# A conv layer's norm shift takes its matmul banks two tiles later, and VectorE's splits and gated products come ahead of its taps

## The chip, the cores and the metric

One core of a Trainium2 chip runs the whole program in one launch. The metric is the time of one execution in microseconds of the device, from a median of several; smaller is better. The engines named below are the PE (TensorE, matrix products), VectorE (DVE), ScalarE (ACT), GpSimd (POOL) and SyncE (SP, which issues the DMAs).

## What is computed

The reference is a network of a recurrent block and four mixer layers (conv, RWKV, attention, conv) on 512 tokens of 1024 channels, with a context of 256 tokens beside it in the first three. The change touches the two conv layers alone. Cut to what matters:

```python
def conv_branch(h, w_in, dw, db, ln_g, ln_b, w_out):
    a, b, gate = jnp.split(h @ w_in, 3, axis=-1)
    y = a * jax.nn.sigmoid(b)
    y = depthwise_conv(y, dw, db)            # 31 taps along the tokens, a filter for each channel
    y = jax.nn.silu(layernorm(y, ln_g, ln_b))
    return (y * jax.nn.silu(gate)) @ w_out
```

The first conv layer (layer 0) has 768 tokens, since the context goes through it too; the last one (layer 3) has 512.

## The kernel before

**Tiles.** In `conv_layer` (L693) channels lie on the 128 partitions, so 1024 channels make eight tiles `kt` = 0 to 7, and tokens run along the free dimension: W = 512 in layer 3, W = 784 in layer 0 (two spans of 256 and 512 with a gap). For each tile there are three projections (`proj`, L752): 1 for `b`, 0 for `a`, 2 for the gate. A projection loads a 1024 x 128 block of weights (`wblock`, L180), splits it into a high part on ScalarE (`whi`, L171) and a low part on VectorE (`wlo`, L174), and makes, for each of eight k, three products (L200, L201, L203) for each span. The raw weights have two buffers, `whi` and `wlo` three each.

**A tile's way.** `gated(kt)` (L762) makes the two projections, and from them y (`ypad`, with zeros at its ends, three buffers) with a tanh on ScalarE (L772) and a gated product on VectorE (L773). The 31 taps then run on VectorE (`conv_dve`, L800: L802 for the first, L805 for thirty more, each adding to the same row `cvo`), or, for the tiles in `PEK` (2, 4, 6, 7 in layer 3; 3, 6, 7 in layer 0), on the PE (`spread`, L776, which copies rows with 16 DMAs, and `conv_pe`, L788). `gate(kt)` (L757) makes the third projection and a silu.

**The shift.** The layer norm's sums are taken of values with a rough mean subtracted. This `shift` is the mean of tile 0's rows over its 128 channels, times the number of tiles over 8: one product of `cvo` with a constant (L809), after tile 0's last tap, copied by ScalarE (L811) and subtracted from each tile (L812, or within L797 for tiles on the PE). `sums_of` (L814) adds up the shifted rows and their squares on the PE, two tiles at a time.

**Order.** The order of each engine's instructions is made when the program is built: a scheduler takes the instructions as the source writes them and places each on its engine when its inputs are there. `high_priority(offset=n)` treats what is in its block as if written n instructions earlier; `wblock` uses `WPRIO` = 200. Tiles of the pool `pmm` (six banks; `self.mm()`, L129) hold all projections, the shift's product and, to the end of the loop, one bank of sums. In a projection a call takes one bank for each span.

**What fills in.** `fill` (L598), called at each `wblock`, reads and multiplies one block of the modulation weights (`mod_mul` L584, `mod_cols` L594; they use another pool of two banks). In layer 0 these belong to later layers. In layer 3 there are none left.

Of the kernel before, what the change touches and what calls it, by code (L numbers as in the profile page):

```python
# [12 lines left out]
AF = mybir.ActivationFunctionType  # L13
ALU = mybir.AluOpType
# [9 lines left out]
KT = D // P  # L24
TILES = [0, 128, 256, 384]
EPS = 1e-6
T3=0
WPRIO = 200
FB=[int(c) for c in "2221122333"]
RB=2  # L30
LB=8
# [11 lines left out]
EXP=[int(c) for c in "0001"]  # L43

NAS=[[int(c) for c in x] for x in "00001121200000 00000101000000 00000010100000".split()]
GL=2

PEK=((2,4,6,7),(3,6,7))

# [21 lines left out]
class K:  # L71
    def __init__(self, tc, ins, taps=None):
        self.tc = tc
        self.nc = tc.nc
        self.ins = ins
        self.taps = taps or {}
        self.es = ExitStack()

    def tap(self, name, ap):
        if name in self.taps:  # L80
            self.nc.sync.dma_start(self.taps[name], ap)
# [98 lines left out]
    def wblock(self, w, k0, kn, c0, nc_, eng="act"):  # L180

        n = kn * nc_
        self.fill()
        with self.tc.high_priority(offset=WPRIO):
            raw = self.raw_w()
            rv = raw[:, :n].rearrange("p (k c) -> p k c", k=kn)
            self.nc.sync.dma_start(rv, w[k0 * P:(k0 + kn) * P, c0:c0 + nc_].rearrange("(k p) c -> p k c", p=P))
            hi, lo = self.split_w(raw[:, :n], n, eng)
        return (hi[:, :n].rearrange("p (k c) -> p k c", k=kn), lo[:, :n].rearrange("p (k c) -> p k c", k=kn))
# [503 lines left out]
    def conv_layer(self, i, X, XC):  # L693
        nc, ins = self.nc, self.ins
        j = i // 3
        gs, sh, ga = self.modulation(i)
        if XC is not None:
            segs = [(XC, 2, 1), (X, 4, 0)]
            spans = [(0, 256), (256, 768)]
            offs, W = [0, 272], 784  # L700
        else:
            segs = [(X, 4, 0)]
            spans = [(0, 512)]
            offs, W = [0], 512
        lens = [b - a for a, b in spans]
        ns = len(segs)
        w_in, w_out = ins["conv_w_in_2"][j], ins["conv_w_out_2"][j]
        with ExitStack() as es:
# [5 lines left out]
            cv = yp.tile([P, KT, W], F32, name="cvo")  # L714
# [7 lines left out]
            ps = self.ptr.tile([P, 512], F32, name="tr")  # L722
# [9 lines left out]
            shift = yp.tile([P, W], F32, name="shift")  # L732
# [15 lines left out]
            with es2:  # L748
                xh, xl = (lambda k: hh[:, k, :]), (lambda k: hl[:, k, :])
                work = self.pool(es2, "cvw", bufs=2)  # L750

                def proj(sec, kt):  # L752
                    ps = [self.mm() for _ in range(ns)]
                    self.linear_fm([ps[q][:, :lens[q]] for q in range(ns)], w_in, sec * D + kt * P, xh, xl, spans)
                    return ps

                def gate(kt):  # L757
                    ps = proj(2, kt)
                    for q in range(ns):
                        nc.scalar.activation(sg[:, kt, offs[q]:offs[q] + lens[q]], ps[q][:, :lens[q]], AF.Silu)  # L760

                def gated(kt):  # L762

                    pb, pa = proj(1, kt), proj(0, kt)
                    yp_ = work.tile([P, W + 32], F32, name="ypad", bufs=3)
                    nc.gpsimd.memset(yp_[:, 0:15], 0.0)  # L766
                    if ns == 2:
                        nc.gpsimd.memset(yp_[:, 271:287], 0.0)
                    nc.gpsimd.memset(yp_[:, W + 15:W + 32], 0.0)
                    for q in range(ns):  # L770
                        y = yp_[:, 15 + offs[q]:15 + offs[q] + lens[q]]
                        nc.scalar.activation(y, pb[q][:, :lens[q]], AF.Tanh, scale=0.5)  # L772
                        nc.vector.scalar_tensor_tensor(y, y, 1.0, pa[q][:, :lens[q]], ALU.add, ALU.mult)  # L773
                    return yp_

                def spread(kt, yp_):  # L776


                    w = work.tile([P, 8, 4, 32], F32, name="wst", bufs=1)
                    nc.vector.tensor_tensor(w, dwq[:, :, :, kt].rearrange("p g m -> p m g").unsqueeze(3).to_broadcast([P, 8, 4, 32]),  # L780
                                            id32.unsqueeze(1).unsqueeze(1).to_broadcast([P, 8, 4, 32]), ALU.mult)
                    y4 = work.tile([P, 4, W + 28], F32, name="y4", bufs=1)
                    for g in range(4):
                        for q in range(4):
                            nc.sync.dma_start(y4[32 * q:32 * q + 32, g, :], yp_[32 * g:32 * g + 32, q:q + W + 28])
                    return y4, w

                def conv_pe(kt, y4, w):  # L788
                    ps = [self.mm() for _ in range(ns)]
                    for q in range(ns):  # L790
                        for m in range(8):
                            for g in range(4):
                                nc.tensor.matmul(ps[q][32 * g:32 * g + 32, :lens[q]], w[:, m, g, :],
                                                 y4[:, g, offs[q] + 4 * m:offs[q] + 4 * m + lens[q]], start=m == 0, stop=m == 7)
                    for q in range(ns):
                        sl = slice(offs[q], offs[q] + lens[q])
                        nc.vector.scalar_tensor_tensor(cv[:, kt, sl], ps[q][:, :lens[q]], self.col("conv_db_2", 8 * j + kt),  # L797
                                                       shift[:, sl], ALU.add, ALU.subtract)

                def conv_dve(kt, yp_):  # L800
                    acc = cv[:, kt, :]
                    nc.vector.tensor_scalar(acc, yp_[:, 0:W], dwh[:, 0, kt:kt + 1], self.col("conv_db_2", 8 * j + kt),  # L802
                                            ALU.mult, ALU.add)
                    for tap in range(1, 31):
                        nc.vector.scalar_tensor_tensor(acc, yp_[:, tap:tap + W], dwh[:, tap, kt:kt + 1], acc, ALU.mult, ALU.add)  # L805
                    if kt == 0:
                        ps = [self.mm() for _ in range(ns)]
                        for q in range(ns):
                            nc.tensor.matmul(ps[q][:, :lens[q]], self.inv_d, acc[:, offs[q]:offs[q] + lens[q]], start=True, stop=True)  # L809
                        for q in range(ns):  # L810
                            nc.scalar.activation(shift[:, offs[q]:offs[q] + lens[q]], ps[q][:, :lens[q]], AF.Copy, scale=float(KT))  # L811
                    nc.vector.tensor_tensor(acc, acc, shift, ALU.subtract)  # L812

                def sums_of(kt):  # L814

                    for q in range(ns):
                        rhs, sl = [], slice(offs[q], offs[q] + lens[q])
                        for k in (kt, kt + 1):
                            sq = work.tile([P, 512], F32, name="sq")
                            nc.scalar.activation(sq[:, :lens[q]], cv[:, k, sl], AF.Square)  # L820
                            rhs += [cv[:, k, sl], sq[:, :lens[q]]]
                        if kt == KT - 2 and ns == 1:

                            nc.scalar.activation(warm, sq[:, 0:1], AF.Sqrt)
                        for i, x in enumerate(rhs):
                            nc.tensor.matmul(sums[q][32 * i:32 * i + 32, :lens[q]], self.inv_d[:, 0:32], x,
                                             start=kt == 0, stop=kt == KT - 2)

                on_pe, ops = PEK[ns - 1], {}
                for kt in range(KT):  # L830
                    yp_ = gated(kt)
                    if kt in on_pe:
                        ops[kt] = spread(kt, yp_)
                    else:
                        conv_dve(kt, yp_)
                    if kt >= GL:
                        gate(kt - GL)
                    if kt - 1 in on_pe:
                        conv_pe(kt - 1, *ops[kt - 1])
                    if kt % 2 and kt > 2:  # L840
                        sums_of(kt - 3)
                gate(KT - 2)
                conv_pe(KT - 1, *ops[KT - 1])
                sums_of(KT - 2)
                gate(KT - 1)

            with ExitStack() as es2:
                op = self.pool(es2, "cvo", side="right")
# [72 lines left out]
    def rwkv_layer(self, X, XC):  # L921
# [133 lines left out]
        def feat(name, i, shape=(P, 384)):  # L1055
            return fp.tile(list(shape), F32, name=name, bufs=FB[i])

# [900 lines left out]
def build(tc, ins, out, taps=None, stages="F0123", test=None):  # L1958
    k = K(tc, ins, taps)
    nc = tc.nc  # L1960
    with k.es:
        k.setup()
        sd = dict(side="right") if stages[0] == "2" else {}
        X = k.open_stream(**sd)
        with tc.high_priority(offset=10 * WPRIO):
            for t in range(4):
# [60 lines left out]
```

## Time and profile before

| | us |
|---|---|
| median of 3 runs | 2747.01 (2746.84 to 2750.37) |
| the profiled execution | 2750.99 |
| its span, first to last instruction | 2749.3 |
| PE busy | 2401.8 (87%) |
| VectorE busy | 1696.3 (62%) |
| ScalarE busy | 1014.8 (37%) |
| GpSimd busy | 713.7 (26%) |
| mean granted PE clock | 0.919 of full speed |

The shares are means over stages with different limits; what the change is worth has to be read from the two conv layers, in time from about 400 to 860 and from about 2450 to the end. Matmuls are pipelined, so a row's duration is longer than the distance to the next row's start; the distance is what counts.

### The profile page before, as it was taken

To read this page: it belongs to the slowest core of one execution; us is meant where nothing else is said; L and a number is where in the kernel's file an instruction comes from. 1 tells how busy PE (TensorE), PEld (TensorE's weight loads), DVE (VectorE), ACT (ScalarE), POOL (GpSimd) and SP (SyncE) were. 2 spreads that over 40 slices of the span, in tenths; PEclk is the share of its full clock that TensorE was granted. 3 is DMA by queue.
4 is the path that set the end of the run, shared out by engine and by line. 5 is a ranking of instruction groups with operands and counts; after the bars stand their busy time and mean duration, and the time that the engine had idled before them with its cause. 6 is when DMAs were issued, how large, how long until landed. Compare 5 with 4: busy or idle time off the path is not lost. (4 is left out here: it accounts for less than half of the span.)

```text
span 2749.3 us, 48387 instructions
## 1 busy us (share of the span) xinstructions
PE 2401.8 (87%) x19837; PEld 1900.0 (69%) x19867; DVE 1696.3 (62%) x2577; ACT 1014.8 (37%) x1861; POOL 713.7 (26%) x700
## 2 busy tenths in 40 slices
PE   6998867999895889888699885989999899996996
PEld 4776655877574767566588774768788788874655
DVE  4434356687357588888778883545154378446836
ACT  4642342212332233233355552233333367331223
POOL 0101001000204269988222531210000287100001
PEclk9998986999997989999599997989999999997998
DMA  5523444224322327665524444432455311221331
GB/s 149 149 81 108 153 131 130 70 71 117 86 69 72 88 62 237 178 190 166 194 95 145 138 134 128 178 113 81 148 152 160 116 47 39 83 79 48 108 94 54
DMA packets 352942, 319.06 MB, mean 116 GB/s; under 512 B 19679, under 2 KB 292032, under 8 KB 352208
## 3 DMA queue, kind: packets, MB, share of 16 engines
q1 hardware_dynamic: 352720, 315.95, 38.1%
q8 instruction: 157, 2.57, 0.4%
q14 instruction: 65, 0.53, 0.1%
HBM read 241.85 MB, written 64.63 MB: 111 GB/s over the span
## 5 line engine op out<-in xcount | busy, mean ns | idle before, releaser
L174 DVE TENSOR_TENSOR wlo<-wraw,whi 128x1024 fp32r<-128x1024 f32 x212 | 267.5, 1263 | 489.6 <-ACT whi L171 478.1
L171 ACT ACTIVATE whi<-wraw 128x1024 fp32r<-128x1024 f32 x212 | 224.3, 1058 | 742.5 <-PE mm L201 404.8
L201 PE MATMUL mm<-hT_lo,whi 128*128 128x512 f32 (+1 forms) x864 | 323.2, 374 | 0.0
L200 PE MATMUL mm<-hT_hi,whi 128*128 128x512 f32 (+1 forms) x864 | 317.8, 379 | 0.8 <-ACT h L679 0.8
L203 PE MATMUL mm<-hT_hi,wlo 128*128 128x512 f32 (+1 forms) x864 | 290.4, 371 | 0.5 <-DVE wlo L174 0.5
L805 DVE SCALAR_TENSOR_TENSOR cvo<-ypad,dwh,cvo 128x784 f32<-128x784 f32 (+1 forms) x270 | 239.3, 908 | 5.6
L203 PEld LDWEIGHTS mm<-hT_hi,wlo 128*128 128x128 f32 x864 | 164.1, 190 | 40.3 <-issue 2.2
L201 PEld LDWEIGHTS mm<-hT_lo,whi 128*128 128x128 f32 x864 | 165.0, 191 | 34.9 <-issue 7.8
L200 PEld LDWEIGHTS mm<-hT_hi,whi 128*128 128x128 f32 x864 | 165.0, 191 | 34.3 <-issue 9.8
L219 PE MATMUL mm<-whi,hT_hi 128*128 128x512 f32 x384 | 152.8, 399 | 1.3 <-ACT hT_hi L264 1.3
L220 PE MATMUL mm<-wlo,hT_hi 128*128 128x512 f32 x384 | 152.4, 397 | 0.0
L221 PE MATMUL mm<-whi,hT_lo 128*128 128x512 f32 x384 | 150.2, 399 | 0.0
L766 POOL MEMSET ypad<- 128x15 f32 x16 | 1.7, 113 | 551.0 <-DVE cvo L805 215.5
L201 PE MATMUL mm<-llo,whi 128*128 128x256 f32 (+1 forms) x256 | 89.3, 370 | 10.1 <-DVE llo L274 10.0
L200 PE MATMUL mm<-lhi,whi 128*128 128x256 f32 (+1 forms) x256 | 82.7, 365 | 17.2 <-POOL lhi L273 16.0
L584 PE MATMUL tr<-mraw,sc 128*32 128x128 f32 x1536 | 72.1, 309 | 28.7 <-DMA mraw<-in_mod_w_dram 25.1
L219 PE MATMUL mm<-whi,lhi 128*128 128x512 f32 x192 | 82.5, 432 | 8.1 <-DVE so L1525 3.9
L220 PE MATMUL mm<-wlo,lhi 128*128 128x512 f32 x192 | 81.2, 423 | 5.8 <-DVE wlo L174 5.8
L219 PEld LDWEIGHTS mm<-whi,hT_hi 128*128 128x128 f32 x384 | 72.7, 189 | 18.7 <-issue 2.2
L220 PEld LDWEIGHTS mm<-wlo,hT_hi 128*128 128x128 f32 x384 | 72.6, 189 | 15.5 <-issue 1.0
L221 PEld LDWEIGHTS mm<-whi,hT_lo 128*128 128x128 f32 x384 | 71.9, 189 | 16.3 <-issue 2.2
L221 PE MATMUL mm<-whi,llo 128*128 128x512 f32 x192 | 79.8, 426 | 2.7 <-DVE llo L274 2.7
(501 smaller groups left out, 5880.4 us busy)
## 6 DMA issues: line engine op xcount, KB each, us to landing
mraw<-in_mod_w_dram SPq DMA_DIRECT2D x96, 512.0 KB
wraw<-in_conv_w_in_dram SPq DMA_DIRECT2D x48, 512.0 KB
wraw<-in_attn_w_in_dram SPq DMA_DIRECT2D x48, 512.0 KB
wraw<-in_w_in_dram SPq DMA_DIRECT2D x24, 512.0 KB
f_d<-F SPq DMA_DIRECT2D x32, 384.0 KB
ar_d<-AR SPq DMA_DIRECT2D x32, 384.0 KB
F<-f_d SPq DMA_DIRECT2D x24, 512.0 KB
AR<-ar_d SPq DMA_DIRECT2D x24, 512.0 KB
```

Of the source, the lines that this page charges most:

```text
L171: nc.scalar.activation(hi[:, :n], raw, AF.Copy)
L174: nc.vector.tensor_tensor(lo[:, :n], raw, hi[:, :n].bitcast(F32), ALU.subtract)
L200: nc.tensor.matmul(ps[s], wh[:, k, :], xh(k)[:, a:b], start=k == 0, stop=False)
L201: nc.tensor.matmul(ps[s], wh[:, k, :], xl(k)[:, a:b], start=False, stop=False)
L203: nc.tensor.matmul(ps[s], wl[:, k, :], xh(k)[:, a:b], start=False, stop=k == kts - 1)
L219: nc.tensor.matmul(ps, h, wh[:, kk, :], start=k == 0, stop=False)
L220: nc.tensor.matmul(ps, h, wl[:, kk, :], start=False, stop=False)
L221: nc.tensor.matmul(ps, l, wh[:, kk, :], start=False, stop=k == kts - 1)
L584: nc.tensor.matmul(ps[g:g + 32, 0:P], self.sc[:, k, :], raw[:, k, :], start=k < 4, stop=k >= 4)
L766: nc.gpsimd.memset(yp_[:, 0:15], 0.0)
L805: nc.vector.scalar_tensor_tensor(acc, yp_[:, tap:tap + W], dwh[:, tap, kt:kt + 1], acc, ALU.mult, ALU.add)
```

## The change

- The shift's product leaves `conv_dve(0)`. A new function `first_shift` makes it behind `gated(2)`, so behind the projections of tiles 1 and 2, one bank for each span in turn; it also subtracts the shift from tiles 0 and 1. `conv_dve` subtracts it itself only for `kt > 1`.
- `gate(0)` moves from `kt` = 2 to `kt` = 1; at `kt` = 2 there is no gate, from 3 on it is `gate(kt - 2)` as before.
- In the loop over `kt` the weight loads and splits have the priority offset 800 (`CPRIO`) in place of 200, and the tanh and the gated product (L772, L773) get it too, which had none.

```diff
+CPRIO = 800
-GL=2
-        with self.tc.high_priority(offset=WPRIO):
+        with self.tc.high_priority(offset=self.wprio):
...
-                    for q in range(ns):
-                        y = yp_[:, 15 + offs[q]:15 + offs[q] + lens[q]]
-                        nc.scalar.activation(y, pb[q][:, :lens[q]], AF.Tanh, scale=0.5)
-                        nc.vector.scalar_tensor_tensor(y, y, 1.0, pa[q][:, :lens[q]], ALU.add, ALU.mult)
+                    with self.tc.high_priority(offset=CPRIO):
+                        for q in range(ns):
+                            y = yp_[:, 15 + offs[q]:15 + offs[q] + lens[q]]
+                            nc.scalar.activation(y, pb[q][:, :lens[q]], AF.Tanh, scale=0.5)
+                            nc.vector.scalar_tensor_tensor(y, y, 1.0, pa[q][:, :lens[q]], ALU.add, ALU.mult)
...
-                    if kt == 0:
-                        ps = [self.mm() for _ in range(ns)]
-                        for q in range(ns):
-                            nc.tensor.matmul(ps[q][:, :lens[q]], self.inv_d, acc[:, offs[q]:offs[q] + lens[q]], start=True, stop=True)
-                        for q in range(ns):
-                            nc.scalar.activation(shift[:, offs[q]:offs[q] + lens[q]], ps[q][:, :lens[q]], AF.Copy, scale=float(KT))
-                    nc.vector.tensor_tensor(acc, acc, shift, ALU.subtract)
+                    if kt > 1:
+                        nc.vector.tensor_tensor(acc, acc, shift, ALU.subtract)
+
+                def first_shift():
+
+                    acc = cv[:, 0, :]
+                    for q in range(ns):
+                        ps, sl = self.mm(), slice(offs[q], offs[q] + lens[q])
+                        nc.tensor.matmul(ps[:, :lens[q]], self.inv_d, acc[:, sl], start=True, stop=True)
+                        nc.scalar.activation(shift[:, sl], ps[:, :lens[q]], AF.Copy, scale=float(KT))
+                    for kt in range(2):
+                        nc.vector.tensor_tensor(cv[:, kt, :], cv[:, kt, :], shift, ALU.subtract)
...
-                on_pe, ops = PEK[ns - 1], {}
+                on_pe, ops, self.wprio = PEK[ns - 1], {}, CPRIO
                 for kt in range(KT):
                     yp_ = gated(kt)
+                    if kt == 2:
+                        first_shift()
                     if kt in on_pe:
                         ops[kt] = spread(kt, yp_)
                     else:
                         conv_dve(kt, yp_)
-                    if kt >= GL:
-                        gate(kt - GL)
+                    if kt == 1 or kt > 2:
+                        gate(max(0, kt - 2))
```

Behind the loop `self.wprio` goes back to 200.

## Rows read from the trace of the kernel before

**Rows 1.** Windows by stage: busy us and count of each engine, clock, DMA.

```profile
core 0: us, PE busy (x) PEld busy (x) DVE busy (x) ACT busy (x) POOL busy (x), PEclk, DMA share, GB/s
443.00:487.00 44.00, 23.61 (x290) 16.46 (x290) 33.96 (x38) 5.09 (x17) 0.20 (x3) 0.53 0.69 195
487.00:735.00 248.00, 248.00 (x1628) 185.31 (x1628) 163.07 (x177) 47.37 (x82) 0.98 (x14) 0.99 0.30 80
2480.00:2510.00 30.00, 3.60 (x49) 3.02 (x38) 27.29 (x35) 3.34 (x5) 0.15 (x2) 0.56 0.13 36
2510.00:2671.00 161.00, 161.00 (x796) 108.95 (x799) 105.63 (x132) 38.22 (x48) 0.63 (x8) 0.99 0.35 98
```

**Rows 2.** Timeline, PE, layer 3: start, us, line, operands, count, [idle before, releaser].

```profile
2479.76 0.65 PE L725 MATMUL tr<-dwh,ident 128*32 128x64 f32 x32
...
2483.42 1.72 PE L639 MATMUL tr<-ident,mod 128*128 128x128 f32 x8 [1.92 <-ACT dwq L727]
2509.62 2.07 PE L809 MATMUL mm<-cvo,inv_d 128*128 128x512 f32 x2 [24.48 <-DVE cvo L805]
```

**Rows 3.** Timeline, ScalarE, layer 3: first and last of the three splits.

```profile
2457.13 1.04 ACT L171 ACTIVATE whi<-wraw 128x1024 fp32r<-128x1024 f32 x1
...
2482.04 1.05 ACT L171 ACTIVATE whi<-wraw 128x1024 fp32r<-128x1024 f32 x1
```

**Rows 4.** Timeline, PE, layer 0: the shift's product.

```profile
486.55 2.93 PE L809 MATMUL mm<-cvo,inv_d 128*128 128x256 f32 x4
```

**Rows 5.** Groups by line, PE, 443.5 to 486.5: busy, mean ns, idle before.

```profile
L584 PE MATMUL tr<-mraw,sc 128*32 128x128 f32 x244 | 16.3, 412 | 18.8 <-DMA mraw<-in_mod_w_dram 16.8 <-DVE mod L595 1.5 <-ACT mrow L585 0.5
L594 PE MATMUL tr<-msel,mrow 128*128 128x2 f32 x32 | 6.7, 330 | 1.6 <-ACT mrow L585 1.6
```

**Rows 6.** Windows of L200 alone: us, PE busy (count), clock, DMA.

```profile
2524.05:2546.36 22.31, 12.63 (x32) 1.00 0.35 92
515.09:548.80 33.71, 20.29 (x64) 1.00 0.22 63
```

**Rows 7.** Timeline, VectorE, layer 3: tile 0's taps; two tiles' taps.

```profile
2485.98 23.59 DVE L805 SCALAR_TENSOR_TENSOR cvo<-ypad,dwh,cvo 128x512 f32<-128x512 f32 x30
...
2555.62 4.07 DVE L805 SCALAR_TENSOR_TENSOR cvo<-ypad,dwh,cvo 128x512 f32<-128x512 f32 x6
```

**Rows 8.** Timeline, VectorE, layer 0: tile 0 alone; tiles 1 and 2.

```profile
444.97 0.68 DVE L802 TENSOR_SCALAR cvo<-ypad,dwh,cols 128x784 f32<-128x784 f32 x1
...
457.40 9.59 DVE L805 SCALAR_TENSOR_TENSOR cvo<-ypad,dwh,cvo 128x784 f32<-128x784 f32 x9
...
526.57 0.68 DVE L802 TENSOR_SCALAR cvo<-ypad,dwh,cols 128x784 f32<-128x784 f32 x1
...
534.03 7.65 DVE L805 SCALAR_TENSOR_TENSOR cvo<-ypad,dwh,cvo 128x784 f32<-128x784 f32 x8
...
570.24 0.97 DVE L812 TENSOR_TENSOR cvo<-cvo,shift 128x784 f32<-128x784 f32 x1
```

**Rows 9.** Windows of L805 alone, layer 0: us, VectorE busy (count).

```profile
508.00:526.50 18.50, 12.40 (x12) 1.00 0.20 58
526.50:570.30 43.80, 34.63 (x36) 1.00 0.38 99
```

**Rows 10.** Groups by line, VectorE: 498 to 676, then 2524 to 2636.

```profile
L174 DVE TENSOR_TENSOR wlo<-wraw,whi 128x1024 fp32r<-128x1024 f32 x19 | 23.2, 1223 | 16.9 <-ACT whi L171 16.7
L773 DVE SCALAR_TENSOR_TENSOR ypad<-ypad,mm 128x256 f32<-128x256 f32 (+1 forms) x14 | 7.2, 552 | 11.5 <-PE mm L203 11.5
...
L174 DVE TENSOR_TENSOR wlo<-wraw,whi 128x1024 fp32r<-128x1024 f32 x16 | 19.6, 1223 | 7.4 <-ACT whi L171 7.2
L773 DVE SCALAR_TENSOR_TENSOR ypad<-ypad,mm 128x512 f32<-128x512 f32 x6 | 4.1, 687 | 5.0 <-PE mm L203 4.6 <-DMA wraw<-in_conv_w_in_dram 0.4
```

**Rows 11.** Timeline, PE, layer 0: a modulation group at full clock.

```profile
644.62 0.64 PE L584 MATMUL tr<-mraw,sc 128*32 128x128 f32 x16
```

**Rows 12.** The page's group of all low-part splits of the kernel.

```profile
L174 DVE TENSOR_TENSOR wlo<-wraw,whi 128x1024 fp32r<-128x1024 f32 x212 | 267.5, 1263 | 489.6 <-ACT whi L171 478.1
```

More of the change, by code (lines that the diff above doesn't have):

```diff
@@ L77, in __init__ @@
         self.es = ExitStack()
+        self.wprio = WPRIO
     def tap(self, name, ap):
@@ L845, in conv_layer @@
                 gate(KT - 1)
+            self.wprio = WPRIO
             with ExitStack() as es2:
```

## The prediction

> **What bounds the kernel now.** I read the busy time by stretch first. In each of the two conv layers it shows the same picture: a stretch in which the PE is nearly idle, and behind it one in which it is never idle [rows 1]. In conv layer 0 the PE is busy 23.61 of the 44 us from 443 to 487 and then 248.00 of 248; in conv layer 3 it is busy 3.60 of 30 us from 2480 to 2510 and then 161.00 of 161. So behind the gap the PE sets the end of the layer, VectorE (163.07 of 248, 105.63 of 161) does not, and a gain can only come from the gap.
>
> Then the PE in order of time. In conv layer 3 the two projections of tile 0 end at 2479.8, some small products follow, and then the PE sits 24.48 us in front of L809, the shift's product, whose releaser is the tap line L805 [rows 2]. Tile 1's projections stand behind it, though their weights are there: three splits had been made beyond tile 0's, the last started at 2482.04 [rows 3]. Nothing else that the profile shows holds them, and at most three of the six banks are taken (one by the sums, two by tile 0). I read it so: a bank of the pool is handed out in the order of the source, so whoever asks behind the shift's product waits until that product is placed, and the PE, which takes its matmuls in order, waits with it. In conv layer 0 the same wait ends with L809 at 486.55 [rows 4]; there the modulation products (L584, L594) fill it, 15 groups of 16 matmuls in 43 us, 23.0 us busy, mostly waiting for their own DMA [rows 5].
>
> **The change, part by part.**
>
> *The product behind two tiles.* In front of it now stand pb1, pa1 (tile 1's projections), gate 0, pb2 and pa2: five projections in either layer. Their pitch is read behind the gap: a projection has eight L200 in layer 3 (one for each k) and sixteen in layer 0 (two spans), and four of them take 22.31 us with 32 L200 and 33.71 us with 64 [rows 6], so 5.58 and 8.43 us each. They are worth 27.9 us and 42.1 us of PE work that leaves the bound stretch. But the product keeps its condition, the last tap of tile 0, and the question is when that comes. Every us that it comes later than 2509.6 or 486.6 is taken off again.
>
> *Tile 0's taps now have company.* Before, VectorE ran them with no other taps around: in layer 3 30 taps from 2485.98 in 23.59 us, 0.786 us each; in layer 0 from L802 at 444.97, 1.07 us each (nine in 9.59) [rows 7, 8]. Where two tiles have taps open, they run turn by turn: in layer 0 tile 1 has 12 of its 30 taps behind it when tile 2's L802 starts at 526.57, and its subtraction L812 comes at 570.24 with 36 taps between, of which it needed 18; so 18 to 18 [rows 8, 9]. Turn by turn the pitch is shorter, 0.95 us (eight in 7.65, of which the last 1.03 is one whole tap) and 0.66 us (six in 4.07, the last 0.75) [rows 7, 8], yet tile 0 gets only half of the turns.
>
> Layer 3: pb1 can start at 2480.4, so pa1 ends at 2491.6 and y1 follows. Until then VectorE has 5.6 us, less one weight split (1.2 us, and 0.46 us of wait before it, 7.4 us over 16 [rows 10]): 3.9 us, 5 taps. 25 remain, with tile 1's between them 50 turns of 0.66 = 33.0. To this come y1 and L802 (1.2), four splits (4.9), y2 (0.7) and the waits (4 x 0.46, and 0.83 for y2, 5.0 us over 6 [rows 10]; 2.7): 2491.6 + 42.5 = 2534.1. The PE's five projections end at 2480.4 + 27.9 = 2508.3, and it then waits some 26 us. The gain is 27.9 - (2534.1 - 2509.6) = 3.4 us.
>
> Layer 0: the five projections and one modulation group with each (0.64 us at full clock [rows 11], with its share of L594 some 0.9) run from 443.6 to 490; pa1 ends at 462. Until then VectorE has 16.3 us less two splits with waits (2 x 2.1; the wait is 16.9 us over 19 [rows 10]): 12.1 / 1.07 = 11 taps. 19 remain, 38 turns of 0.95 = 36.1; y1 and L802 1.8, four splits 8.4, y2 with its wait of 1.6 and its L802 3.4: 462 + 49.7 = 511.7. Of the 15 modulation groups five run with the projections and (511.7 - 490) / 2.8 = 7 in the wait that is left, at the gap's own 2.8 us each [rows 5]; three move into the bound stretch, 2.7 us. The gain is 42.1 - (511.7 - 486.6) - 2.7 = 14.3 us.
>
> Bounds. Tile 2's taps come in at 490 in layer 0; the trace shows no three tiles at once. If three take turns, the 8 that tile 0 has left take 8 x 0.95 longer: 7.6 us, gain 7 there. If tile 0 has right of way and others only fill (18 of 36 speaks against it), the product comes at 2491.6 + 25 x 0.786 + 9 = 2520.3 and at 462 + 19 x 1.07 + 9 = 491, gains 17 and 42.1 - 4.4 - 9 (ten groups move) = 29. I take turns of two, the one that rows show: 3.4 + 14.3, **18 us**.
>
> *Splits and gated products ahead of taps.* In the bound stretches the PE waits for no split now (161.00 of 161, 248.00 of 248 [rows 1]). So this earns nothing by itself; it is the cover for the first part, as VectorE now has up to 60 taps queued while the PE asks for weights every 5.58 us. Queued behind such an instruction are tile 0's taps, and behind them the product and the PE: see the rival below. The added cost of L812 for tile 0 and 1 is none: the same count, off the path, their reader is the sums a tile later. The weight DMAs move ahead of the modulation loads and of the 16 row copies of a spread tile on SP; three split weights stand ready at the gap's start [rows 3], and the PE, never idle behind it, has not waited for a load either [rows 1]; I count nothing.
>
> *Banks.* In layer 0 the five projections take ten banks of five that go round, so pb2 needs pa1's, freed by y1 on VectorE. In the bound stretch the same round costs the PE nothing [rows 1]; I count 0, at most the 1.6 us that VectorE waits at a tile's product (11.5 us over 14 halves of 7 tiles [rows 10]). The Trainium skill (Perfetto Trace Analysis, Optimization Strategy) says that a repeated gap on the engine that should be full can mean too little PSUM for the next tile. By that the gap would stay where it is and the gain be 0; the trace speaks against it, since it ends with a tap and not with a release.
>
> *Clock.* The granted clock is 0.53 and 0.56 of 2.4 GHz in the gaps, so nearly all at the lower level, 1.2 GHz, and 0.99 behind, at the upper [rows 1]. A wait of some 20 us stays in both layers, so the slow first projection stays; 0.
>
> The sum: 18 us. The profiled execution has 2749.3 us of span and 2751.0 in all, 4.0 above the median of 2747.0. On its own scale the forecast is 2733; against the median it is 2747 - 18 = 2729.
>
> **The rivals.**
>
> *The product is hidden, or nearly.* Tile 0's taps keep the right of way, and the PE meets the product at 2520 and 491: gain 17 + 29 = 46, 2701 us. For it: the splits and products now come first and take the other tile's turns. Against it: the 18 to 18 held although splits came in between. 0.22.
>
> *Nothing is gained.* The product comes only when both tiles' taps are nearly done: 55 turns of 0.66 for layer 3, 2491.6 + 45.8 = 2537.4, gain nothing; in layer 0 49 turns, 462 + 60 = 522, gain 5. Also here belongs that the wait merely moves and something later in the layer is late. 2740 to 2747 us. For it: three tiles at once in layer 0. 0.16.
>
> *Slower.* VectorE's own order turns against the taps: a split stands ahead of tile 0's taps and waits for its ScalarE half, which waits until the PE frees a slot; the taps behind it stand still. In the sum I gave each split 0.46 and 0.89 us of wait; over the whole kernel 489.6 us lie in front of 212 splits, 2.3 each [rows 12]. Eleven splits stand in the two sums, so the gain of 18 is gone when each waits 1.6 us more; at twice the kernel's mean (4.6) they wait some 43 us more and the time is 2729 + 43 = 2772 us. Against it: in the stretches with taps the waits were short. 0.08. The Trainium skill (TensorE: Matmul & The Clock Gate, Architectural detail) calls VectorE's queue strictly first in, first out; the waits of [rows 10] agree.
>
> **How the numbers follow.** Forecast (two tiles in turn, with the three-tile bound) 0.54, from 2718 to 2738; hidden 0.22; nothing 0.16; slower 0.08. The time is the forecast's, 2729. The range has to leave out no more than two in ten: it runs from 2700, the hidden case, to 2743, some of the case with nothing gained. A measurement of this kernel tells 0.2%, 5.5 us, from no change. Faster by more than that: the forecast, the hidden case and a little of the third, 0.78; within: 0.13; slower: 0.09.
>
> **What would show it.** In the changed profile the PE's wait in front of L809's successor (the shift's product) should stand behind five projections, about 26 us long in layer 3 and about 22 in layer 0 with modulation groups in it; tile 0's last tap near 2534 and 512 on the old scale; the stretches behind the product without PE idle time and shorter by 28 and 39 us. If the wait is under 10 us, the right of way was mis-read; if tile 0's taps end past 2537 and 523, the change loses. If the PE still sits in front of tile 1's projections, my reading of the banks is wrong.

## The result

The changed kernel takes 2717.14 us (median of 4 runs, 2710.93 to 2723.18), the kernel before 2748.02 (4 runs, 2746.84 to 2750.37): a ratio of 0.9886, 95% interval 0.9861 to 0.9912, or 30.9 us less. The forecast was 18 us less, 2729 (2700 to 2743). The profiled execution of after took 2723.18 us with a span of 2721.5, so it is the slowest of its four.

In after, the shift's product is L816 (was L809), its subtraction L819, a tile's first tap L804 (L802), the other taps L807 (L805), the gated product y L775 (L773), a weight's low part L175 (L174), the modulation products L585 and L595 (L584, L594), the sums L833.

From the records of both executions I set four marks in each conv layer: the start of the first projection, of the shift's product, of the first product of the statistics behind the sums, and the end of the layer's last product. The stretches between them, in us:

| | before | after | difference |
|---|---|---|---|
| layer 0: first projection to shift's product | 64.84 | 82.28 | +17.4 |
| layer 0: shift's product to statistics | 246.21 | 209.62 | -36.6 |
| layer 0: statistics to end | 93.21 | 93.48 | +0.3 |
| layer 3: first projection to shift's product | 42.66 | 58.17 | +15.5 |
| layer 3: shift's product to statistics | 167.86 | 137.56 | -30.3 |
| layer 3: statistics to end | 63.18 | 62.77 | -0.4 |

The two layers give back 34.1 us. The rest of the program, which the change doesn't touch, took 6.3 us more in this execution of after than in that of before, which leaves the 27.8 us by which the spans differ.

Windows of after by stage answer [rows 1] (us from start to end, their length, busy us and count of each engine, granted clock, DMA share, GB/s):

```profile
core 0: us, PE busy (x) PEld busy (x) DVE busy (x) ACT busy (x) POOL busy (x), PEclk, DMA share, GB/s
443.00:487.00 44.00, 44.00 (x326) 36.92 (x319) 39.01 (x43) 10.31 (x18) 0.00 (x0) 1.00 0.42 119
496.30:507.00 10.70, 5.28 (x68) 3.68 (x61) 10.70 (x13) 1.11 (x4) 0.03 (x1) 0.53 0.76 204
507.00:716.60 209.60, 209.60 (x1501) 151.28 (x1502) 136.37 (x148) 37.63 (x72) 1.15 (x17) 0.99 0.37 100
2463.90:2496.30 32.40, 32.40 (x177) 26.33 (x176) 29.85 (x40) 12.15 (x14) 0.00 (x0) 1.00 0.34 98
2496.34:2512.55 16.21, 0.01 (x2) 0.03 (x1) 16.21 (x25) 0.00 (x0) 0.24 (x4) 0.63 0.39 101
2512.55:2650.10 137.55, 135.56 (x698) 87.68 (x698) 84.96 (x105) 32.45 (x43) 0.54 (x8) 0.98 0.32 90
```

The 44 us of layer 0 in which the PE was busy for 23.61 are now full, at a granted clock of 1.00 of 2.4 GHz and not 0.53. What is left of the gap stands behind the five projections, which end near 492.7. From there it is 14.3 us to the product, and modulation products fill a little under half of them (the window shows the last 10.7). In layer 3 the PE is busy for all of 32.4 us, and 16.2 us of idle time are left. The stretches behind the product are still full.

The timeline of after on the PE (start, us, line, operands, count, idle before and its releaser), layer 3 and then layer 0, answers [rows 2, 4, 5]:

```profile
2463.86 0.65 PE L726 MATMUL tr<-dwh,ident 128*32 128x64 f32 x32
...
2494.40 1.95 PE L640 MATMUL tr<-ident,mod 128*128 128x128 f32 x16
2512.55 1.19 PE L816 MATMUL mm<-cvo,inv_d 128*128 128x512 f32 x1 [16.20 <-DVE cvo L807]
...
492.69 0.95 PE L595 MATMUL tr<-msel,mrow 128*128 128x2 f32 x8
495.96 0.64 PE L585 MATMUL tr<-mraw,sc 128*32 128x128 f32 x16 [2.32 <-DVE mod L596]
...
502.11 1.08 PE L585 MATMUL tr<-mraw,sc 128*32 128x128 f32 x16 [3.97 <-DMA mraw<-in_mod_w_dram]
...
507.00 2.91 PE L816 MATMUL mm<-cvo,inv_d 128*128 128x256 f32 x4
```

The wait in front of the product is 16.20 us where it was 24.48, and its releaser is a tap of VectorE as before. The forecast had some 26 us here, and some 22 in layer 0, where 14.3 are left. The product now comes at 2512.55, after all five projections and L640.

### The profile page after: what moved, and what is told of

It is laid out like the page before. It is cut to its first block, busy times and chain, and to the rows that moved or that the text cites. A ratio compares the mean times of both kernels' runs of the same rounds, so it can differ in the third digit from the quotient of the medians.

```text
span 2721.5 us, 48392 instructions
## 1 busy us (share of the span) xinstructions
PE 2398.6 (88%) x19837; PEld 1900.8 (70%) x19867; DVE 1693.8 (62%) x2577; ACT 1014.6 (37%) x1861; POOL 714.7 (26%) x700
## 5 line engine op out<-in xcount | busy, mean ns | idle before, releaser
L175 DVE TENSOR_TENSOR wlo<-wraw,whi 128x1024 fp32r<-128x1024 f32 x212 | 268.0, 1265 | 461.9 <-ACT whi L172 446.3
L807 DVE SCALAR_TENSOR_TENSOR cvo<-ypad,dwh,cvo 128x784 f32<-128x784 f32 (+1 forms) x270 | 236.4, 905 | 4.5
L201 PE MATMUL mm<-lhi,whi 128*128 128x256 f32 (+1 forms) x256 | 83.5, 369 | 16.8 <-POOL lhi L274 15.6
L585 PE MATMUL tr<-mraw,sc 128*32 128x128 f32 x1536 | 68.2, 295 | 18.1 <-DMA mraw<-in_mod_w_dram 14.0
L1287 ACT ACTIVATE Df<-ps 32x128 f32<-32x128 f32 x176 | 68.1, 387 | 37.5 <-PE ps L1280 35.2
```

The source lines that it names most:

```text
L175: nc.vector.tensor_tensor(lo[:, :n], raw, hi[:, :n].bitcast(F32), ALU.subtract)
L201: nc.tensor.matmul(ps[s], wh[:, k, :], xh(k)[:, a:b], start=k == 0, stop=False)
L585: nc.tensor.matmul(ps[g:g + 32, 0:P], self.sc[:, k, :], raw[:, k, :], start=k < 4, stop=k >= 4)
L1287: nc.scalar.activation(s.Df[rows, :, :, gsl].rearrange("p t a u -> p u a t"), p3[rows, :, 32 * b:32 * b + 32].rearrange("p u (a t) -> p u ...
```

## The experiments

The theory after the result: the PE's wait comes from the product's bank, which is handed out in the order of the program; the five projections in front of it fill the PE; and what takes part of that back is that tile 0's taps share VectorE with tile 1's from y1 on, so that the product comes later. The rivals: the priorities did it; something other than the shared VectorE sets the product's time; each projection that is moved simply gains its length. The kernel before had a median of 2749.47 us beside the first four runs and of 2749.72 us beside the last three.

### The order without the priorities

```diff
-                    with self.tc.high_priority(offset=CPRIO):
+                    with self.tc.high_priority(offset=0):
...
-                on_pe, ops, self.wprio = PEK[ns - 1], {}, CPRIO
+                on_pe, ops, self.wprio = PEK[ns - 1], {}, WPRIO
```

> The changed kernel with its old priorities: the shift's product stands behind the projections of tiles 1 and 2, but weight splits keep the offset 200 and the tanh and gated product have none. Theory (the five projections in front of the product are the whole gain): as the changed kernel, 2717 us, within 3 us; the idle time in front of the product in layer 3 again 16 us. Rival (the priorities let splits and products in between the taps, and the gain needs them): the PE waits for splits or for tile 1's product within the five projections, and the time lies between 2725 and 2748 us.

Measured: 2718.83 us (2710.11 to 2724.24, 4 runs), ratio to before 0.9894 (0.9878 to 0.9910). The timeline on the PE:

```profile
2499.40 1.19 PE L816 MATMUL mm<-cvo,inv_d 128*128 128x512 f32 x1 [16.20 <-DVE cvo L807]
```

The same idle time to the hundredth, the same 58.18 us from the first projection to the product, and the whole gain. The place of the product is enough.

### The priorities without the order

The kernel before, with the new priorities of weight splits and gated products:

```diff
-        with self.tc.high_priority(offset=WPRIO):
+        with self.tc.high_priority(offset=self.wprio):
...
+                    with self.tc.high_priority(offset=CPRIO):
...
-                on_pe, ops = PEK[ns - 1], {}
+                on_pe, ops, self.wprio = PEK[ns - 1], {}, CPRIO
```

> The kernel before with the new priorities alone (offset 800 for the weight splits of the loop, and for tanh and gated product). Theory: the wait of 24.5 us in layer 3 and of 43 us in layer 0 stays, since the product still takes its banks ahead of tile 1's projections: 2748 us, within 4 us. Rival (the priorities bring part of the gain): 2730 to 2740 us, with a shorter wait.

Measured: 2748.77 us (2744.25 to 2754.07, 11 runs), ratio 0.9996 (0.9986 to 1.0005). The PE's timeline in layer 3:

```profile
2511.51 2.08 PE L812 MATMUL mm<-cvo,inv_d 128*128 128x512 f32 x2 [25.05 <-DVE cvo L808]
```

The wait is there as before, 25.05 us. The priorities earn nothing by themselves, and without them the order loses nothing.

### Another bank for the product, nothing moved

The kernel before, with the shift's product in a bank of the other pool:

```diff
-                        ps = [self.mm() for _ in range(ns)]
+                        ps = [self.ptr.tile([P, 512], F32, name="tr") for _ in range(ns)]
```

> The kernel before with one change: the shift's product is written to a tile of the two-bank pool of the transposes and not to one of the pool of the projections; it stays where it is in the source. Theory (what holds tile 1's projections is only that the product, written ahead of them, has not yet taken its bank of their pool): the PE goes on with tiles 1 and 2 in layer 3, no wait of over 5 us until tile 3's product wants a free row buffer; at least five projections run ahead of the product, and the time is 2715 us or less (the changed kernel's 2717 or better), in layer 0 less gain, as the modulation products use the same two banks. Rival (they are held by something else, weights or the order of the source on the PE): the wait of 24 us in layer 3 stays and the time is 2748 us.

Measured: 2687.51 us (2681.35 to 2691.53, 4 runs), ratio 0.9772 (0.9754 to 0.9789). The PE's timeline in layer 3:

```profile
2501.45 0.40 PE L200 MATMUL mm<-hT_hi,whi 128*128 128x512 f32 x1
2501.69 1.02 PE L809 MATMUL tr<-cvo,inv_d 128*128 128x512 f32 x2
```

Windows from the first projection to the statistics, in layer 0 and in layer 3:

```profile
421.55:701.86 280.31, 278.43 (x2070) 210.50 (x2071) 198.94 (x224) 57.71 (x105) 4.61 (x23) 1.00 0.39 107
2423.68:2609.40 185.72, 184.37 (x915) 121.62 (x915) 131.11 (x179) 48.02 (x61) 4.41 (x15) 0.99 0.33 92
```

This is the edit that settles the cause. In the program, the product stands where it always stood. It comes 78.0 us behind the first projection of layer 3, 35 us later than in before, and the kernel is 2.3% faster, since projections run right up to it. The same two windows of before:

```profile
421.71:732.75 311.04, 290.65 (x2070) 218.16 (x2071) 202.43 (x224) 57.05 (x105) 4.46 (x23) 0.92 0.35 96
2466.96:2677.48 210.52, 182.13 (x914) 123.15 (x914) 138.39 (x179) 48.21 (x61) 4.39 (x15) 0.92 0.29 81
```

And of after:

```profile
424.72:716.62 291.90, 284.16 (x2071) 213.48 (x2072) 201.50 (x224) 56.41 (x105) 4.61 (x23) 0.97 0.38 103
2454.38:2650.10 195.72, 177.53 (x914) 121.54 (x914) 135.78 (x179) 47.89 (x61) 4.42 (x15) 0.96 0.31 88
```

The PE is not busy for 20.4 + 28.4 = 48.8 us of them in before, 25.9 in after and 3.2 with the other bank. So the change took about half of the idle time away, and one bank takes away nearly all.

### More work in front of the product

The changed kernel, with as many further gates in front of the product as are free: gates 1 to 3 in layer 3, gates 1 and 2 in layer 0.

```diff
                     if kt == 2:
+                        early = [1, 2, 3][:4 - ns]
+                        for g in early:
+                            gate(g)
                         first_shift()
...
-                    if kt == 1 or kt > 2:
+                    if kt == 1 or kt > 2 and kt - 2 not in early:
```

> The changed kernel with more gate projections in front of the shift's product: gates 1 to 3 in layer 3, gates 1 and 2 in layer 0, which need nothing of the taps; the gates that follow later are fewer by these. Theory (what is left of the gain is the PE's wait for tile 0's last tap, 16.2 us in layer 3 and some 14 us, partly filled, in layer 0): three projections take 16.8 us of the wait in layer 3 while each split puts the product off by 1.2 us, so the wait falls to some 3 us and the gain there is 13 us; in layer 0 the wait goes but for the modulation groups, gain some 8 us; together 21 us, 2696 us. Rival (VectorE becomes the bound, as its taps now have less projections beside them later): the PE waits later for tile 3's or tile 4's rows, and the time is 2710 to 2725 us.

Measured: 2689.41 us (2686.76 to 2691.41, 4 runs), ratio 0.9780 (0.9766 to 0.9793). The PE's timeline in layer 3:

```profile
2487.88 1.95 PE L640 MATMUL tr<-ident,mod 128*128 128x128 f32 x16
2492.97 1.10 PE L816 MATMUL mm<-cvo,inv_d 128*128 128x512 f32 x2 [3.14 <-DVE cvo L807]
```

The product comes 61.8 us behind the first projection, 3.6 later than in after, while three projections of 5.6 us more stand in front: the wait falls from 16.20 to 3.14 us. A gate needs no tap, so this filling brings VectorE no new company. It ends where the other bank ended, by another way and with the pool that was there; I had expected 7 us less of it.

### Tile 0 without company on VectorE

The changed kernel with tile 1's taps given to the PE, in place of tile 2's in layer 3 and tile 3's in layer 0:

```diff
-PEK=((2,4,6,7),(3,6,7))
+PEK=((1,4,6,7),(1,6,7))
...
-                    for kt in range(2):
+                    for kt in range(1):
```

> The changed kernel, with tile 1's taps given to the PE in both layers (in place of tile 2's in layer 3 and tile 3's in layer 0), so that tile 0 has VectorE to itself until tile 2's y comes; the subtract behind the product then takes tile 0 alone. Theory (what sets the product's time behind five projections is the company on VectorE: from tile 1's first tap on, tile 0 gets every second tap): in layer 3 the 31 taps of tile 0 end about 25 us behind its first one (30 x 0.79) and not 42.7, so the product comes some 44 us behind the first projection and not 58.2, and the PE's idle in front of it falls from 16.2 us to 0 to 5; in layer 0 the product comes right behind the fifth projection, some 69 to 73 us behind the first one and not 82.3, and the modulation groups that stood in front of it move behind it. Together 20 us less than the changed kernel's 2717: 2697, within 2690 to 2708, if the taps that are now tile 2's and 3's cost the rest of the stage nothing. Rival (something else than the company, such as the splits or the tanh, sets the product's time): product and idle stay, 2712 to 2722.

Measured: 2694.61 us (2690.56 to 2696.91, 4 runs), ratio 0.9801 (0.9785 to 0.9817). VectorE's timeline in layer 3, from tile 0's first tap to tile 2's:

```profile
2446.18 0.54 DVE L804 TENSOR_SCALAR cvo<-ypad,dwh,cols 128x512 f32<-128x512 f32 x1
2446.75 3.90 DVE L807 SCALAR_TENSOR_TENSOR cvo<-ypad,dwh,cvo 128x512 f32<-128x512 f32 x5
...
2472.48 0.54 DVE L804 TENSOR_SCALAR cvo<-ypad,dwh,cols 128x512 f32<-128x512 f32 x1
```

The PE's timeline at the product:

```profile
2481.59 1.19 PE L816 MATMUL mm<-cvo,inv_d 128*128 128x512 f32 x1 [8.71 <-DVE cvo L807]
```

The time came as expected. In layer 0 the product stands 66.6 us behind the first projection, right behind the five, without a wait. In layer 3 the wait fell to 8.71 us and not to 0 to 5. I had left out the splits that VectorE makes between the taps, and the last six taps of tile 0 ran in turn with tile 2's, whose first tap came at 2472.48. The product stands 35.4 us behind tile 0's first tap, where it was 42.7 in after. From the first projection it comes 7.5 us sooner than in after (50.7 and 58.2) in layer 3 and 15.7 us sooner in layer 0. So the company delays it; in layer 3 the splits between the taps do too, and they stay.

### Only one tile in front

The changed kernel with the product behind tile 1's projections: pb1 and pa1 are in front, gate 0, pb2 and pa2 behind. Tile 1's subtraction goes back into `conv_dve` (not shown).

```diff
...
-                    if kt == 2:
+                    if kt == 1:
                         first_shift()
...
-                    if kt == 1 or kt > 2:
-                        gate(max(0, kt - 2))
+                    if kt > 1:
+                        gate(kt - 2)
```

> The changed kernel, with the shift's product behind one more tile's projections and not two: pb1 and pa1 stand in front of it, gate 0 and tile 2's behind it. Theory (two effects of opposite sign: each projection in front fills the PE, but tile 1's y starts a company on VectorE that delays the product): tile 1's y is there, so the product comes as late as in the changed kernel, 58 us behind the first projection in layer 3 (15.5 later than before), while only two projections (11.2 us) have come in front: idle in front of the product about 29 us and not 24.5 or 16.2, and layer 3 some 4 us longer than before. In layer 0 tile 2's taps don't come in, 14 taps stand ahead of tile 1's first one and 34 turns behind it: product some 76 us behind the first projection, 11 later than before, with 16.9 us of projections moved: up to 6 us won. Sum: 2746, within 2740 to 2752. Rival (each projection that moves in front gains its share of the 31 us, without a price to pay first): two of five, 2735.

Measured: 2740.75 us (2738.81 to 2742.76, 7 runs), ratio 0.9969 (0.9958 to 0.9980). VectorE's timeline in layer 3, at tile 1's first tap and behind it:

```profile
2481.34 0.54 DVE L804 TENSOR_SCALAR cvo<-ypad,dwh,cols 128x512 f32<-128x512 f32 x1
...
2482.93 29.49 DVE L807 SCALAR_TENSOR_TENSOR cvo<-ypad,dwh,cvo 128x512 f32<-128x512 f32 x44
```

The PE's timeline at the product:

```profile
2510.24 2.08 PE L816 MATMUL mm<-cvo,inv_d 128*128 128x512 f32 x2 [28.49 <-DVE cvo L807]
```

Two of the five projections earn 9 of the 31 us, not 12, and all of it in layer 0 (8.0 us less from the first projection to the layer's end). In layer 3 the wait is 28.49 us, longer than in before, though 11 us of work were put in front: layer 3 ends 0.4 us sooner. I had expected it 4 us later. The time alone lies halfway between my 2746 and the rival's 2735; it is layer 3, where two projections in front earn next to nothing, that speaks against the rival. The price is paid once, when tile 1's taps start: after has three projections more in front (16.8 us), its product comes only 3.2 us later (58.2 and 55.0 us behind the first projection), and its layer 3 is 14.8 us shorter.

### The changed kernel with the other bank

```diff
-                        ps, sl = self.mm(), slice(offs[q], offs[q] + lens[q])
+                        ps, sl = self.ptr.tile([P, 512], F32, name="tr"), slice(offs[q], offs[q] + lens[q])
```

> The changed kernel, with the product's banks from the other pool, as was done to the kernel before (2687.5 us). Theory (the wait of the PE in front of the product was all that either kernel lost, and it came from banks handed out in the order of the program): with the banks free the place of the product in the program doesn't matter any more, the PE has no idle in front of it in either layer, and the time is that of the kernel before with the free banks: 2687, within 2681 to 2693. Rival (the reorder and the priorities bring something of their own on VectorE, which the wait hid): 2665 to 2680. Second rival (the product put back by two tiles costs when nothing waits for it): above 2695.

Measured: 2687.93 us (2685.76 to 2691.14, 4 runs), ratio 0.9778 (0.9764 to 0.9793), against 0.9772 for the other bank alone. Windows from the first projection to the statistics:

```profile
422.92:701.00 278.08, 278.08 (x2070) 213.09 (x2071) 198.91 (x224) 56.09 (x105) 4.47 (x23) 0.99 0.40 108
2427.32:2614.55 187.23, 185.88 (x915) 121.74 (x915) 132.19 (x179) 47.54 (x61) 4.40 (x15) 0.99 0.33 92
```

With the bank free, the reorder adds nothing. Both rivals fall, and the one-line edit of the bank is as good as any combination tried: 2687.5 us, 30 below the changed kernel.

## Why the prediction was right, and where its sizes were off

**What bounds the kernel.** Right, and shown by the runs: the gap is the PE's wait for the product's bank, and the gain comes from it. The reading that banks are handed out in the order of the program is shown by the run with another bank, which left the product in its place and took the wait away. The Trainium skill (Perfetto Trace Analysis, Optimization Strategy) offers too little PSUM as a possible cause of a gap that repeats. The runs speak against it as the cause here: the reorder kept the same pool and fills 32.4 us of layer 3, and with early gates all but 3.14 us.

**The sum.** The mechanism was right in both layers, the size was not. By the marks of the table above, with the prediction's terms (us of gain, losses negative):

| term | forecast | measured |
|---|---|---|
| layer 3: the stretch behind the product | 27.9 | 30.3 |
| layer 3: the product comes later | -24.5 | -15.5 |
| layer 0: the stretch behind the product, modulation groups taken off | 42.1 - 2.7 | 36.6 |
| layer 0: the product comes later | -25.1 | -17.4 |
| both layers: the stretch behind the statistics | 0 | 0.1 |
| sum | 18 | 34.1 |

So the stretches behind the product were right within 3 us each. What was mis-sized, by 9.0 and 7.7 us, is when the product comes. VectorE's timeline of layer 3 in after shows it:

```profile
2469.89 0.55 DVE L804 TENSOR_SCALAR cvo<-ypad,dwh,cols 128x512 f32<-128x512 f32 x1
2470.47 3.11 DVE L807 SCALAR_TENSOR_TENSOR cvo<-ypad,dwh,cvo 128x512 f32<-128x512 f32 x4
2473.50 1.22 DVE L175 TENSOR_TENSOR wlo<-wraw,whi 128x1024 fp32r<-128x1024 f32 x1
2474.63 3.10 DVE L807 SCALAR_TENSOR_TENSOR cvo<-ypad,dwh,cvo 128x512 f32<-128x512 f32 x4
2477.88 0.69 DVE L775 SCALAR_TENSOR_TENSOR ypad<-ypad,mm 128x512 f32<-128x512 f32 x1
2478.48 0.75 DVE L807 SCALAR_TENSOR_TENSOR cvo<-ypad,dwh,cvo 128x512 f32<-128x512 f32 x1
2479.14 0.54 DVE L804 TENSOR_SCALAR cvo<-ypad,dwh,cols 128x512 f32<-128x512 f32 x1
2479.60 1.22 DVE L175 TENSOR_TENSOR wlo<-wraw,whi 128x1024 fp32r<-128x1024 f32 x1
2480.74 4.06 DVE L807 SCALAR_TENSOR_TENSOR cvo<-ypad,dwh,cvo 128x512 f32<-128x512 f32 x6
...
2494.68 0.69 DVE L775 SCALAR_TENSOR_TENSOR ypad<-ypad,mm 128x512 f32<-128x512 f32 x1 [0.28 <-PE mm L204]
...
2497.08 18.34 DVE L807 SCALAR_TENSOR_TENSOR cvo<-ypad,dwh,cvo 128x512 f32<-128x512 f32 x27
```

*Taps done before company.* The forecast gave tile 0 five taps before y1 and left 25, so 50 turns, 33.0 us. In after 8 are done when y1 comes and a ninth before tile 1's first tap. From then to the product there are 41 taps, 21 of tile 0 and 20 of tile 1: in turn, as forecast (the rows don't name the tile; 41 is the count that turns give), and 42 turns in all, 27.7 us at 0.66. The reason for the early start: in before tile 0's first L805 came 19.0 us behind the first projection (2485.98 in [rows 7], 2466.96), in after 16.1. VectorE's rows ahead of the taps, in before and then in after:

```profile
2482.18 0.69 DVE L773 SCALAR_TENSOR_TENSOR ypad<-ypad,mm 128x512 f32<-128x512 f32 x1 [0.69 <-ACT ypad L772]
...
2484.27 1.22 DVE L780 TENSOR_TENSOR wst<-dwq,id 128x1024 f32<-128x1024 f32 x1
2485.40 0.54 DVE L802 TENSOR_SCALAR cvo<-ypad,dwh,cols 128x512 f32<-128x512 f32 x1
```

```profile
2467.01 1.23 DVE L782 TENSOR_TENSOR wst<-dwq,id 128x1024 f32<-128x1024 f32 x1 [0.96 <-ACT dwq L728]
2468.15 0.68 DVE L775 SCALAR_TENSOR_TENSOR ypad<-ypad,mm 128x512 f32<-128x512 f32 x1
```

About half of the 2.9 us is that tile 0's y comes 1.4 us sooner behind the first projection (15.2 and 13.8 us): that projection ran at the upper clock level in after (see the end), which is luck as far as the runs tell and shifts tile 1's y as well. The other half is the copy of the PE's tap weights (L780, now L782), which stood between y and the first tap and now stands ahead of y; so it does in every kernel here but the two in which the PE waits in front of tile 1's projections. This half leaves tile 0 more room before y1, 7.4 us and not 5.6. I had taken the start of before as fixed and didn't ask what a new order on VectorE does to it.

*Waits.* I gave four splits 0.46 us each and y2 0.83 us, the means of [rows 10]. In after the four splits between tile 1's first tap and the product wait for nothing (the first of them stands above), and y2 0.28: 2.4 us less. Eight turns fewer (5.3 us), these waits and the 1.1 us by which y1 came sooner, which goes with the luck above, make 8.8 of the 9.0 us.

Layer 0 goes the same way. VectorE's timeline in after:

```profile
457.27 7.46 DVE L807 SCALAR_TENSOR_TENSOR cvo<-ypad,dwh,cvo 128x784 f32<-128x784 f32 x7
465.20 1.02 DVE L775 SCALAR_TENSOR_TENSOR ypad<-ypad,mm 128x256 f32<-128x256 f32 x2 [0.48 <-PE mm L204]
...
468.22 0.68 DVE L804 TENSOR_SCALAR cvo<-ypad,dwh,cols 128x784 f32<-128x784 f32 x1
...
484.44 1.23 DVE L175 TENSOR_TENSOR wlo<-wraw,whi 128x1024 fp32r<-128x1024 f32 x1 [0.21 <-ACT whi L172]
...
496.77 0.68 DVE L804 TENSOR_SCALAR cvo<-ypad,dwh,cols 128x784 f32<-128x784 f32 x1
497.37 10.48 DVE L807 SCALAR_TENSOR_TENSOR cvo<-ypad,dwh,cvo 128x784 f32<-128x784 f32 x11
```

y1 came 40.5 us behind the first projection, forecast 40.3. Four splits behind it took 4.8 us, not 8.4, since only one waited, 0.21 us; y2 with its wait and its first tap took 2.0, not 3.4. Of the turns, 17 were left to tile 0, not 19.

**The bound of three tiles.** It happened, and it cost little. At tile 2's first tap (496.77) tile 0 has 26 taps behind it: 6 and 7 before y1, one more before tile 1's, and 12 of the 24 between 468.81 and 496.77. Its last four take ten taps until the product at 507.00, where turns of two would have taken eight: 1.9 us, not 7.6, since only four taps were left.

**Modulation products.** I let three groups of 16 move behind the product of layer 0. Seven did. The window of that line alone behind the product, in before and then in after (us, PE busy with its count, weight loads, clock, DMA):

```profile
486.55:732.75 246.20, 5.11 (x100) 3.04 (x96) 0.99 0.30 81
```

```profile
507.00:716.60 209.60, 9.90 (x208) 5.98 (x208) 0.99 0.37 100
```

That is 13 groups where 6 were, and at the forecast's 0.9 us each 6.3 us and not 2.7: 42.1 - 6.3 = 35.8, measured 36.6. The two errors go together: the product came sooner, so fewer groups fitted in front of it. In layer 3 the stretch shrank by 2.4 us more than the five projections; 2.0 of them lie in the products of the sums, whose 32 matmuls keep the PE busy for 10.4 us where it was 12.4. Why they overlap better wasn't tried.

**Counted at nothing.** The priorities: shown to be nothing, by either run. The banks' round in layer 0: the PE is busy for all of the 44 us from 443 to 487. The weight loads: no wait for one shows there.

**The rivals.** Tile 0's right of way falls: 21 and 20 taps in turn. Nothing gained falls with the time. Slower, by splits that wait in front of tile 0's taps, was no part of it: 0.21 and 0 us, not the 1.6 us each from which it would have decided. The Trainium skill (TensorE: Matmul & The Clock Gate, Architectural detail) has VectorE's queue as strictly first in, first out. The rows agree as far as they go: no tap starts past the one split that waits, for 0.21 us.

**The two signs.** That the product's delay is taken off again, which carried the sum, is shown from both ends: with one tile in front the delay eats all of the gain in layer 3, and with tile 1's taps off VectorE the changed kernel gains 22.5 us more.

## What to carry to other kernels

Where an engine in order waits in front of an instruction whose operand is late, ask who handed it its place: a buffer of another pool for that one instruction was worth 62 us here, twice what this change brought. Moving work in front came as far only with work that needs nothing of the engine waited for (the early gates, 60 us). If work is moved in front, price what it starts elsewhere: in one layer the first tile in front paid all of its gain for the company that its taps gave to the ones waited for, and the next tile's projections came nearly free. And when a step is timed from a trace of before, ask whether the change moves its start too, as here, where one copy out of the way and a wait less let tile 0 finish 3 more taps before its company came.

## What the runs showed of the hardware

*Idle time and busy time fall together, and the clock is a part of it.* From the first projection to the statistics the same matmuls (2070 or 2071, and 914 or 915) keep the PE busy for 472.8 us in before, 461.7 in after and 462.8 with the other bank, at a granted clock of 0.92, 0.97 or 0.96, and 0.99 or 1.00. So of the 33.9 us that after gained there, 22.9 are idle time, and 11.1 are the same work in less time. Of these 11.1, 6.6 lie in layer 0's modulation products, which take 363 and 302 ns each (L584, L594) in before and 296 and 262 in after. There the clock shows: the 44 us of the gap had 0.53 in before [rows 1] and have 1.00, the upper level of 2.4 GHz, in after. A group of 16 took 1.08 us in the stretch of after with a clock of 0.53 (502.11 above), and 0.64 at full clock [rows 11]. Some 1.5 us lie in the first projection of layer 3: 7.3 us in before, with a clock of 0.50 in its first 3.1 us, and 5.8 at 1.00 in after. It varied between the kernels run here (5.8 to 8.5), and what sets the level there stays open. But 2.0 us lie in the sums, whose matmuls last as long as before (597 and 595 ns) and only overlap more. Nor does the clock alone set the busy time: with tile 1's taps on the PE it is 457.3 us at 1.00 and 0.97, less than with the other bank. The forecast had counted the clock as nothing beside the wait; its terms held this part all the same, as they went by stretches and not by idle time.

*The same order, 14 us apart.* Executions of after and of the order without priorities went from 2710.1 to 2724.2 us, at a mean granted clock of 0.931 to 0.924, by and large the lower the longer. In the two profiled ones, whose spans are 13.2 us apart, most of the difference lies outside the conv layers: between layer 0's end and layer 3's first projection 1636.2 us stand against 1644.3, and ahead of layer 0 421.3 against 424.7. What decides this isn't settled by these runs.
